# Hybrid decoder step on one core: output projection and first norm by single token groups, and two fixed PSUM banks for the inner down projections

## The chip, the core and the metric

The kernel runs on one core of one Trainium2 chip. The metric is the device time of one execution in microseconds (us). Before the change it is 2619.73 us, the median of 3 runs (2619.33 to 2625.12). The engines are named as in the profile: PE (TensorE matmul), PEld (its weight loads), DVE (VectorE), ACT (ScalarE), POOL (GpSimd), SP (SyncE, which issues most DMAs).

## The reference, cut to what matters

One layer of a decoder: an input projection, sliding-window attention beside an mLSTM, and then the part that this change touches, for 2048 prompt tokens and 64 sample tokens of width 1024 (the inner width of the FFN is 2816):

```python
def mix_and_ffn(x, att, h_m, o_pre, ...):
    o = jax.nn.sigmoid(o_pre).reshape(h_m.shape)
    y = jnp.concatenate([head_norm(att, g_attn), head_norm(o * h_m, g_mlstm)], axis=-1)
    x1 = layer_norm(DEEPNORM_ALPHA * x + y @ w_out, ln1_g, ln1_b)      # output projection, first norm
    ffn = (jax.nn.silu(x1 @ w_gate) * (x1 @ w_up)) @ w_down            # gate, up and down projection
    return layer_norm(DEEPNORM_ALPHA * x1 + ffn, ln2_g, ln2_b)         # second norm
```

Every matmul is done in float32 accuracy from split operands: a value is the sum of a rounded high part and a low part, and a product is three matmuls (high x high, high x low, low x high).

## The kernel before, in words

**Tiles.** Activations lie with the features on the 128 partitions (8 feature tiles, `KD`) and the tokens along the free axis. The 2112 tokens are cut into 4 *pairs* of *token groups*; a group has 256 tokens in pairs 0 and 1 and 272 in pairs 2 and 3 (`WH`), so a pair is 512 or 544 wide (`W2`). A pair is what the FFN works on: gate and up projection are done by one Strassen step, whose 2x2 right-hand matrix has the two groups of the pair as its columns and the two halves of the features as its rows. Its seven products P1 to P7 need the operands B11 (first features, first group), B21 (last features, first group), B22 (last features, second group) and the sums T1 to T4, which mix both groups. P1 needs B11 alone and P2 B21 alone; P3 needs B22; P4 to P7 need T4, T1, T2 and T3.

**Stages of one pair.** (1) `out_proj(g, m)`, m = 0 to 7: the output projection of feature tile m, 24 matmuls for each column range; a pair of 512 is one column range in one PSUM bank, a pair of 544 is two of 272. DVE adds the product to the residual (L1140), and POOL sums the eight tiles for the mean (L1125, L1127). (2) `ln1(g)`: the first norm. A mean by one matmul (L1151), subtraction (L1157, DVE), squares (L1159, ACT) and their sums, a reciprocal root (small DVE steps between L497 and L509 on PE), scaling (L1172, DVE), the bias (L1212, ACT), and then the Strassen operands, each split in high (L133, ACT) and low part (L142, DVE). For a pair of 512 all of it runs over the whole pair; for 544 the statistics run twice, one column half after the other, both after the eight products. (3) Strassen gate and up projection in 11 steps of two products sets, with (4) `down` between: after every 4 of the 22 inner tiles (`SLICES`) the down projection of those tiles is added to the residual (L1331), 8 feature tiles at a time; the last slice has 6 tiles. (5) `ln2`: the second norm and the output, run in the background of the next pair's first products.

**Weights.** `wblock` brings a 128x512 block of weights by one DMA (256 KB) on SP's queue, and ACT (L133) and DVE (L142) split it. `run` asks for five blocks ahead of the item in hand (`LOOK`), and there are 12 buffers for split weights and 5 for raw ones.

**PSUM.** Products of this part use four banks: two with the tag "ga", one "gb", one "gc". `gps()` deals them out in turn ("ga", "gb", "ga", "gc"). The Strassen products hold "ga", "gb" and "gc" by name, and when an inner `down` runs, P3 and P4 of the last set are still to come, so that one "ga" bank and "gc" hold sums that wait for them.

**Order.** At the end of pair g the items stand so: `begin(g + 1)` (loads of the residual and of the mixer's output Y), `out_proj(g + 1, 0)`, P3 and P4 of the last set, `out_proj(g + 1, 1..7)`, then the eight `down` items of the last slice of pair g, and behind each of them one or two steps of the generator `ln1(g + 1)` (`LSTEP`); what is left of it is drained behind the last `down`. For pair 0 there is no earlier pair: `out_proj(0, 0..7)`, the whole `ln1(0)`, then five "late" tiles of the input projection, which do not depend on it. The mixer (attention and mLSTM) of later tokens runs as a background queue between the products (`pace`, `bg_step`). Instructions are then put in order engine by engine by a scheduler that simulates the program as it is built; every engine executes its own list in that order.

## Time and profile before

| what | value |
|---|---|
| runs shown | 2619.73 us median (2619.33 to 2625.12) |
| profiled execution, its own time | 2622.01 us |
| its span on the core | 2619.6 us |
| PE busy | 2445.0 us (93%), 16383 matmuls |
| PE weight loads | 2234.3 us (85%) |
| DVE busy | 1688.2 us (64%) |
| ACT busy | 1171.4 us (45%) |
| POOL busy | 365.1 us (14%) |
| mean granted TensorE clock | 0.97 |
| HBM read, written | 339.26 MB, 68.06 MB |

The busy time of PE has a modelled end for each matmul, so that rows of neighbouring matmuls overlap: the distance from start to start says more of their cost than the duration does. A row such as `L145 PE MATMUL gps<-x,w` is one of the three matmuls of a split product (L145, L146, L147); `x` are the operands of the output projection and of gate and up, `h` those of the down projection. What stands in square brackets in a timeline row is the idle time of the engine before it and what ended it.

### The profile page before, as it was taken

Reading aid. Unit: us, or ns where it says so; the run is one execution under the profiler, and the core shown is the slowest. Engines: PE = TensorE matmul, PEld = TensorE weight load, DVE = VectorE, ACT = ScalarE, POOL = GpSimd, SP = SyncE. Lnnn points to the kernel's source line nnn. Section 1 sums busy time; section 2 is a strip of 40 time slices with the busy share of each in tenths; the row PEclk is TensorE's granted clock in tenths of the full one; section 3 lists DMA queues with packets and bytes.
Section 4 is the critical chain, followed back from the end, with each engine's and each line's share of the span. In section 5 each row is a group of like instructions: output and inputs, shape, how many; then the busy total and the mean of one; then the engine's idle time right before and its main releaser. Section 6 shows DMA issues by size and latency. Waiting matters only on the chain.

```text
span 2619.6 us, 44985 instructions
## 1 busy us (share of the span) xinstructions
PE 2445.0 (93%) x16383; PEld 2234.3 (85%) x16383; DVE 1688.2 (64%) x3956; ACT 1171.4 (45%) x2533; POOL 365.1 (14%) x391
## 2 busy tenths in 40 slices
PE   8999899977899999998999999789999998899996
PEld 8999777756888888878888899688999998899996
DVE  5224443555767766778766776866667748666666
ACT  3112433544454555545555463443444625454454
POOL 3322333202000000041000003110000021100002
PEclk9999999978999999999999999899999998999998
DMA  8643766642555555424655563256444623444453
GB/s 292 219 159 133 243 225 195 214 159 91 168 161 153 161 154 159 151 83 141 223 150 149 157 184 109 84 184 171 130 123 140 189 83 98 126 146 141 142 149 111
DMA packets 302712, 409.30 MB, mean 156 GB/s; under 512 B 31442, under 2 KB 172842, under 8 KB 302474
## 3 DMA queue, kind: packets, MB, share of 16 engines
q1 hardware_dynamic: 260240, 351.54, 44.7%
q10 hardware_dynamic: 42250, 54.89, 5.8%
q8 instruction: 128, 2.10, 0.3%
q14 instruction: 94, 0.77, 0.1%
HBM read 339.26 MB, written 68.06 MB: 155 GB/s over the span
## 4 chain that ended last, share of the span: by engine, by line
PE 45%; DVE 4%; DMA 3%; ACT 2%; issue 1%; POOL 1%; ACTq 0%; SPq 0%; DVEq 0%; POOLq 0%
PE gps L145 14%; PE gps L146 13%; PE gps L147 13%; DVE z L1172 1%; PE bps L571 1%; DMA P<-GW 1%; DMA x<-YD 1%; DVE w L142 1%; ACT w L133 1%; DVE z L1331 1%; DVE z L1157 0%; POOL ft L1164 0%; DMA out_oS<-P 0%; PE bps L596 0%; DMA z<-in_xT 0%
## 5 line engine op out<-in xcount | busy, mean ns | idle before, releaser
L133 ACT CAST w<-wr 128x512 fp32r<-128x512 f32 (+1 forms) x898 | 543.6, 611 | 842.3 <-PE gps L146 746.6
L145 PE MATMUL gps<-x,w 128*128 128x272 f32 (+3 forms) x2968 | 866.3, 301 | 55.9 <-ACT x L133 27.1
L146 PE MATMUL gps<-x,w 128*128 128x272 f32 (+3 forms) x2968 | 873.3, 297 | 7.3 <-DVE x L142 7.1
L147 PE MATMUL gps<-x,w 128*128 128x272 f32 (+3 forms) x2968 | 861.7, 296 | 2.5 <-DVE w L142 2.5
L142 DVE TENSOR_TENSOR w<-wr,w 128x512 fp32r<-128x512 f32 (+1 forms) x898 | 634.9, 714 | 217.9 <-ACT w L133 189.7
L145 PEld LDWEIGHTS gps<-x,w 128*128 128x128 f32 x2968 | 559.4, 191 | 87.5 <-ACT x L133 34.0
L146 PEld LDWEIGHTS gps<-x,w 128*128 128x128 f32 x2968 | 565.9, 191 | 20.4 <-DVE x L142 11.3
L147 PEld LDWEIGHTS gps<-x,w 128*128 128x128 f32 x2968 | 560.6, 191 | 14.3 <-DVE w L142 3.7
L145 PE MATMUL gps<-h,w 128*128 128x272 f32 (+1 forms) x1056 | 348.0, 333 | 21.1 <-DVE z L1331 13.8
L146 PE MATMUL gps<-h,w 128*128 128x272 f32 (+1 forms) x1056 | 342.2, 325 | 0.2 <-DVE h L142 0.2
L147 PE MATMUL gps<-h,w 128*128 128x272 f32 (+1 forms) x1056 | 341.3, 325 | 0.0
L145 PEld LDWEIGHTS gps<-h,w 128*128 128x128 f32 x1056 | 198.9, 189 | 46.9 <-DVE z L1331 20.8
L1331 DVE SCALAR_TENSOR_TENSOR z<-z,gps 128x272 f32<-128x272 f32 (+1 forms) x240 | 123.1, 518 | 146.4 <-PE gps L147 145.7
L147 PEld LDWEIGHTS gps<-h,w 128*128 128x128 f32 x1056 | 199.3, 189 | 15.7 <-issue 0.2
L146 PEld LDWEIGHTS gps<-h,w 128*128 128x128 f32 x1056 | 200.2, 190 | 13.5 <-DVE h L142 0.4
L142 DVE TENSOR_TENSOR x<-x 128x426 fp32r<-128x426 f32 (+3 forms) x72 | 51.6, 717 | 121.8 <-ACT x L133 102.2
L703 POOL TENSOR_SCALAR_AFFINE_SELECT P<-P 128x512 f32<-128x512 f32 x16 | 15.7, 979 | 808.3 <-DMA P<-GW 709.4
L1127 POOL TENSOR_TENSOR zs<-zs,z 128x512 f32<-128x512 f32 (+2 forms) x58 | 83.5, 1441 | 128.5 <-DVE z L1140 57.5
L196 POOL TENSOR_TENSOR st<-sa 128x256 f32<-128x256 f32 x88 | 66.3, 774 | 218.0 <-DMA SW<-st 181.4
L1164 POOL TENSOR_TENSOR ft<-ft 128x272 f32<-128x272 f32 (+1 forms) x56 | 60.7, 1083 | 254.2 <-ACT ft L1159 201.6
L133 ACT CAST x<-x 128x426 fp32r<-128x426 f32 (+3 forms) x72 | 42.1, 585 | 107.6 <-DMA x<-in_xT 59.1
L1125 POOL TENSOR_TENSOR zs<-z 128x512 f32<-128x512 f32 (+2 forms) x10 | 13.1, 1314 | 498.5 <-DVE z L1331 258.4
(340 smaller groups left out, 3600.5 us busy)
## 6 DMA issues: line engine op xcount, KB each, us to landing
wr<-SW SPq DMA_DIRECT2D x352, 256.0 KB, 2.8
wr<-in_wd SPq DMA_DIRECT2D x168, 256.0 KB, 2.9
wr<-in_wg SPq DMA_DIRECT2D x132, 256.0 KB, 2.7
wr<-in_wu SPq DMA_DIRECT2D x132, 256.0 KB, 2.8
SW<-st ACTq DMA_DIRECT2D x44, 512.0 KB, 5.3
wr<-in_wo SPq DMA_DIRECT2D x64, 256.0 KB, 2.9
sa<-in_wg SPq DMA_DIRECT2D x22, 512.0 KB, 4.8
sa<-in_wu SPq DMA_DIRECT2D x22, 512.0 KB, 4.7
```

Source lines behind the costliest of these rows:

```text
L133: A.copy(out, src)
L142: return veng.tensor_tensor(out=lo, in0=src, in1=hi.bitcast(F32), op=ALU.subtract)
L145: PE.matmul(out, lhsT=wh, rhs=xh, start=start, stop=False, **kw)
L146: PE.matmul(out, lhsT=wh, rhs=xl, start=False, stop=False, **kw)
L147: PE.matmul(out, lhsT=wl, rhs=xh, start=False, stop=stop, **kw)
L196: G.tensor_tensor(out=t[:, i], in0=x, in1=y, op=op)
L571: PE.matmul(s[g][:, j, 0:nk], lhsT=x[r, 2 * tt + j, :], rhs=y[r, 0:nk], start=(i == 0), stop=(i == 2))
L703: G.affine_select(out=gm, in_=gm, pattern=[[0, 4], [1, 128]], compare_op=ALU.is_ge, fill=BIG, base=0, channel_multiplier=-1)
L1127: G.tensor_tensor(out=s[:, c], in0=s[:, c], in1=z[m][:, c], op=ALU.add)
L1164: (V if len(qs) > 1 else G).tensor_tensor(out=q, in0=q, in1=t[:, 0:w], op=ALU.add)
L1172: return V.scalar_tensor_tensor(out=z[k][:, c], in0=z[k][:, c], scalar=Q[:, col + k:col + k + 1], in1=ry[:, 0:c.stop - c.start], op0=ALU.m ...
L1331: V.scalar_tensor_tensor(out=zm, in0=zm, scalar=ALPHA if s == 0 else 1.0, in1=p, op0=ALU.mult, op1=ALU.add)
```

## The change

The unit of the output projection and of the first norm becomes the single token group. `load_y`, `out_proj` and the statistics of `ln1` take one group (256 or 272 columns). All eight feature tiles of the first group are projected, then Y of the second group is loaded (`second`) and `ln1` is created; the eight tiles of the second group follow, with the steps of `ln1` for the first group behind them. The last-slice `down` items carry the rest, two steps each. A `wo` block that served a whole pair is now loaded and split once for each group. Y and the operands B11, B21 and B22 of a group keep their high and low part in one buffer. In `down`, the inner slices (`then` is None) alternate between the tags "ga" and "gb", and no longer take "gc".

```diff
-LSTEP = [2, 1, 1, 1, 1, 1, 2, 2]
+LSTEP = [2, 1, 1, 1, 1, 1, 1, 0]
...
-        def load_y(g):
-            c0, w = F0[g], W2[g]
+        def load_y(g, i):
+            c0, w = F0[g] + i * WH[g], WH[g]
             out = []
             for k in range(KD):
-                raw, h, l = x_tile(F32), x_tile(), x_tile()
+                raw, t = x_tile(F32), x_tile()
                 SP.dma_start(out=raw[:, 0:w], in_=YD[:, k, c0:c0 + w])
-                split("a", h[:, 0:w], l[:, 0:w], raw[:, 0:w])
+                h, l = t[:, 0:w], t[:, HW:HW + w]
+                split("a", h, l, raw[:, 0:w])
                 out.append((h, l))
...
-        def out_proj(g, m, fast=False):
+        def out_proj(g, i, m, fast=False, then=None):
             def fn(wa, wb):
-                z, y, s = P[g]["z"], P[g]["y"], P[g]["s"]
-                for o, n in cols(W2[g]):
-                    c = slice(o, o + n)
-                    p = gps()
-                    ys = [(h[:, c], l[:, c]) for h, l in y]
-                    product(p[:, 0:n], wa, ys[0:4], True, False)
-                    product(p[:, 0:n], wb, ys[4:8], False, True)
-                    V.scalar_tensor_tensor(out=z[m][:, c], in0=z[m][:, c], scalar=ALPHA, in1=p[:, 0:n],
-                                           op0=ALU.mult, op1=ALU.add)
+                z, y, s = P[g]["z"], P[g]["y"][i], P[g]["s"]
+                c = half(g, i)
+                p = gps()[:, 0:WH[g]]
+                product(p, wa, y[0:4], True, False)
+                product(p, wb, y[4:8], False, True)
+                V.scalar_tensor_tensor(out=z[m][:, c], in0=z[m][:, c], scalar=ALPHA, in1=p,
+                                       op0=ALU.mult, op1=ALU.add)
                 if not fast or m < KD - 1:
-                    add_to(s, z, m, slice(0, W2[g]))
+                    add_to(s, z, m, c)
+                if then is not None:
+                    then()
...
-            cc = [slice(o, o + n) for o, n in cols(W2[g])]
-            for i, c in enumerate(cc):
...
-            for k in range(4):
-                for kk in (k, k + 4):
-                    scale(z, kk, cc[-1], ry, Q_L1G)
...
+            for c in (a, b):
                 ry = yield from norm(z, c, P[g]["s"], gps, fast)
...
+                for k in range(KD):
+                    scale(z, k, c, ry, Q_L1G)
+                    A.activation(out=z[k][:, c], in_=z[k][:, c], func=AF.Identity, bias=Q[:, Q_L1B + k:Q_L1B + k + 1])
+                    if c is a:
+                        hl1("B11" if k < 4 else "B21", x1[k], k % 4, z[k][:, a])
...
                 hl2("U", k, t[:, 0:2 * w], ("T3", "T4"))
+                hl1("B22", x1[8 + k], k, z[k + 4][:, b])
...
-                    p = gps()[:, 0:c.stop - c.start]
+                    turn[0] += 1
+                    p = (gps() if then else gtag("ga" if turn[0] % 2 else "gb"))[:, 0:c.stop - c.start]
...
+        def second(g):
+            P[g]["y"].append(load_y(g, 1))
...
-            out_proj(0, m, True)
...
+            out_proj(0, 0, m, True)
+        ln0 = [None]
+
+        def begin_ln0():
+            second(0)
+            ln0[0] = ln1(0, True)
+        item(begin_ln0)
+        for m in range(KD):
+            out_proj(0, 1, m, True, step(ln0, LSTEP[m]))
...
-                out_proj(g + 1, 0)
+                out_proj(g + 1, 0, 0)
                 strassen(prev, "P3")
                 strassen(prev, "P4")
                 for m in range(1, KD):
-                    out_proj(g + 1, m)
+                    out_proj(g + 1, 0, m)
 
                 def tails(g=g, lngen=lngen):
-                    P[g]["zs"] = zsum()
+                    second(g + 1)
                     lngen[0] = ln1(g + 1)
                 item(tails)
                 for m in range(KD):
-                    down(g, s, m, cc, True, KD, step(lngen, LSTEP[m]))
+                    out_proj(g + 1, 1, m, False, step(lngen, LSTEP[m]))
+
+                def tails2(g=g):
+                    P[g]["zs"] = zsum()
+                item(tails2)
+                for m in range(KD):
+                    down(g, s, m, cc, True, KD, step(lngen, 2))
```

Three places show how the change moves instructions. The first is DVE's list at the boundary into pair 1. `z_...` are the residual tiles, `gps_...` the PSUM tiles, `w_...` the split weights. Before, the last product of the projection is added at full width, the first `down` product (L1331) follows, and only then the subtraction of the mean (L1157) begins:

```order
L1140 SCALAR_TENSOR_TENSOR z_11102<-z_11102,gps_11500 128x512
L142 TENSOR_TENSOR w_11530<-wr_11528,w_11529 128x256
L142 TENSOR_TENSOR w_11536<-wr_11534,w_11535 128x512
L1331 SCALAR_TENSOR_TENSOR z_5156<-z_5156,gps_11540 128x512
L142 TENSOR_TENSOR w_11607<-wr_11605,w_11606 128x256
L1157 TENSOR_TENSOR z_11088<-z_11088,gps_11588 128x512
```

Now the subtraction for the first group (L1162 in the new numbering) stands among the additions of the second group's products (L1143) and their weight splits:

```order
L1162 TENSOR_TENSOR z_11528<-z_11528,gps_12051 128x256
L142 TENSOR_TENSOR w_12070<-wr_12068,w_12069 128x512
L1143 SCALAR_TENSOR_TENSOR z_11516<-z_11516,gps_12080 128x256
L142 TENSOR_TENSOR w_12076<-wr_12074,w_12075 128x512
L1143 SCALAR_TENSOR_TENSOR z_11518<-z_11518,gps_12134 128x256
L142 TENSOR_TENSOR w_12124<-wr_12122,w_12123 128x512
L1169 TENSOR_TENSOR ft_12108<-ft_12108,ft_12111 128x256
L142 TENSOR_TENSOR w_12130<-wr_12128,w_12129 128x512
```

The norm of the first group has moved ahead of the `down` items and shares DVE with the second half of the projection.

The second place is PE's list where the last reciprocal root of the first norm is spread over the partitions (L509), at the boundary into pair 3. Before, the last `down` product stands ahead of it and Strassen products of the new pair (operands `x`) directly behind it:

```order
L147 MATMUL gps_24162<-h_23144,w_23971 128x272
L1151 MATMUL bps_24632<-zs_23603,avg_80 128x272
L509 MATMUL gps_24183<-C_76,rs_24116 128x68 x4
L145 MATMUL gps_24266<-x_23656,w_23976 128x272
L145 MATMUL gps_24366<-x_23656,w_24261 128x272
```

Now `down` products (operands `h`) stand behind it; nine of them, 18 matmuls each, follow that row (three of 512 columns at the boundaries into pairs 1 and 2):

```order
L147 MATMUL gps_25100<-h_24113,w_24932 128x272
L509 MATMUL gps_25075<-C_76,rs_25008 128x68 x4
L145 MATMUL gps_25162<-h_23452,w_24937 128x272
L146 MATMUL gps_25162<-h_23453,w_24937 128x272
L147 MATMUL gps_25162<-h_23452,w_24938 128x272
```

The work that PE has left when the norm's last factor is known has moved from none to nine products there.

The third place is an inner `down` of pair 3 on PE. Before, 4 of its 16 products stand among the next Strassen products, since their bank comes free only behind P3 or P4; one of them, between two Strassen products:

```order
L147 MATMUL gps_25290<-x_23671,w_25218 128x272
L145 MATMUL gps_25032<-h_24566,w_24872 128x272
L146 MATMUL gps_25032<-h_24567,w_24872 128x272
L147 MATMUL gps_25032<-h_24566,w_24873 128x272
L145 MATMUL gps_25032<-h_24609,w_24872 128x272
```

Now the products follow each other, here the end of one and the beginning of the next:

```order
L146 MATMUL gps_23014<-h_22932,w_22893 128x272
L147 MATMUL gps_23014<-h_22931,w_22894 128x272
L145 MATMUL gps_23028<-h_22542,w_22893 128x272
L146 MATMUL gps_23028<-h_22543,w_22893 128x272
L147 MATMUL gps_23028<-h_22542,w_22894 128x272
```

They alternate between one "ga" bank and "gb".

43 lines of the change are left out of this document (18 added, 25 removed).

## The prediction

> **What bounds the kernel now.** I read the page first, then tables by stage, then the waits of PE in the stages that are not full. The page's engine rows and its chain of work (PE's part is its first number):
>
> ```profile
> PE 2445.0 (93%) x16383; PEld 2234.3 (85%) x16383; DVE 1688.2 (64%) x3956; ACT 1171.4 (45%) x2533; POOL 365.1 (14%) x391
> PE 45%; DVE 4%; DMA 3%; ACT 2%; issue 1%; POOL 1%; ACTq 0%; SPq 0%; DVEq 0%; POOLq 0%
> ```
>
> PE is full over most of the span, so time can come only from where it is not. The tables by stretch (start:end, length, busy of PE, PEld, DVE, ACT, POOL, granted clock, DMA share, GB/s) show where: pair 0's projection and norm, and the three boundaries into pairs 1, 2 and 3.
>
> ```profile
> 505.00:563.00 58.00, 41.83 (x200) 28.30 (x196) 32.22 (x127) 23.04 (x63) 1.71 (x2) 0.74 0.34 104
> 563.00:622.00 59.00, 54.26 (x246) 40.88 (x247) 37.69 (x94) 26.90 (x63) 11.89 (x8) 1.00 0.60 195
> 622.00:662.00 40.00, 17.47 (x81) 15.61 (x80) 29.72 (x64) 20.53 (x38) 4.42 (x3) 0.70 0.13 39
> 1098.00:1129.00 31.00, 31.00 (x134) 25.07 (x134) 13.62 (x19) 6.66 (x13) 9.22 (x6) 1.00 0.28 81
> 1129.00:1160.00 31.00, 31.00 (x142) 25.01 (x142) 24.36 (x44) 11.42 (x22) 11.45 (x8) 1.00 0.32 91
> 1160.00:1200.00 40.00, 30.41 (x185) 26.67 (x185) 38.40 (x69) 23.50 (x45) 13.52 (x3) 0.87 0.29 91
> 1640.00:1700.00 60.00, 44.53 (x237) 37.72 (x237) 51.04 (x117) 28.37 (x57) 9.07 (x8) 0.80 0.25 76
> 2110.00:2180.00 70.00, 70.00 (x569) 69.61 (x567) 42.30 (x95) 19.83 (x42) 24.91 (x25) 1.00 0.28 83
> 2180.00:2220.00 40.00, 29.41 (x198) 27.24 (x197) 35.34 (x82) 23.76 (x45) 2.52 (x3) 0.83 0.31 93
> ```
>
> In each boundary PE is idle while DVE is nearly full (38.40 of 40 us), and in the stretch before it DVE is half idle (13.62 of 31 us) under a full PE. What PE waits for there, by the waits of PE in 622:662, 1640:1700, 2180:2220, and over the whole span, then in two inner down projections of pair 3 (2256:2284, 2410:2424):
>
> ```profile
> PE bps L145 <- ACT ev L939: 15.8, 1, 15.8
> ...
> PE gps L145 <- ACT x L133: 7.2, 3, 5.5
> ...
> PE gps L145 <- ACT x L133: 5.6, 2, 4.9
> ...
> PE gps L145 <- DVE z L1331: 13.9, 27, 2.1
> ...
> PE gps L145 <- DVE z L1331: 4.2, 4, 2.1
> ...
> PE gps L145 <- DVE z L1331: 1.6, 3, 0.5
> ```
>
> The first is a late tile whose bank ACT empties only behind the whole norm; the next two are Strassen operands that the norm has not made yet; the last three are products that wait until DVE has emptied their PSUM bank.
>
> **The change part by part.**
>
> *Pair 0.* Before, the projection needs all of Y of 512 tokens. These rows are the last Y written of the first 256 tokens and of the second, the first and last read of it, the split of the last, then the norm's subtraction, its scaling, and ACT's release of the late tile:
>
> ```profile
> 475.51 0.46 SPq L655 DMA_DIRECT2D YD<-ys  x1
> 574.66 0.38 SPq L655 DMA_DIRECT2D YD<-ys  x1
> 578.43 0.33 SPq L1106 DMA_DIRECT2D x<-YD  x1
> 588.92 0.43 SPq L1106 DMA_DIRECT2D x<-YD  x1
> 592.46 0.69 DVE L142 TENSOR_TENSOR x<-x 128x512 fp32r<-128x512 f32 x1 [2.30 <-ACT x L133]
> 628.40 4.87 DVE L1157 TENSOR_TENSOR z<-z,gps 128x512 f32<-128x512 f32 x8 [1.68 <-PE gps L1154]
> 645.91 5.36 DVE L1172 SCALAR_TENSOR_TENSOR z<-z,Q,gps 128x512 f32<-128x512 f32 x8 [2.17 <-PE gps L509]
> 661.01 1.21 ACT L939 ACTIVATE ev<-bps,C 128x424 f32<-128x424 f32 x2
> ```
>
> Now the first group's eight products (192 matmuls) use Y of 256 tokens, of which the last was written at 475.5; four of them stand ahead of the mixer's last steps in 505 to 563, where PE idles 16 us. Y of the second group needs 16 buffers instead of 24 of the 22, so that its four last reads need not follow each other at 3.5 us (578.43 to 588.92 in three steps): I put the last split at 586 instead of 593. From there DVE's list up to the second norm holds 26 us of work (26 splits, 16 additions and subtractions of 256, 8 scalings, one reciprocal root), and I add 4 us of waits: the second norm begins at 616 instead of 628.4, a gain of 12. From there to ACT's release the trace takes 32.6 us; at half width the subtraction costs 8 x 0.36 instead of 8 x 0.61 us, the scaling 8 x 0.42 instead of 8 x 0.67, the squares and splits some 2 us less: a gain of 6. Together 18 us. The late tiles and first Strassen products behind it are the same work. Bounds: 6, if the four early products (96 matmuls at 0.118, 11.3 us) delay the mixer by what does not fit its gaps; 28, if the 15.8 us wait goes with the 12.
>
> *Narrower matmuls.* A pair of 512 columns had 192 matmuls of 512 and has 384 of 256; pairs 2 and 3 keep theirs at 272. First and last row of a run of each (93 and 46 steps), in output projection and gate:
>
> ```profile
> 600.53 0.40 PE L147 MATMUL gps<-x,w 128*128 128x512 f32 x1
> ...
> 621.99 0.39 PE L147 MATMUL gps<-x,w 128*128 128x512 f32 x1
> ...
> 678.47 0.28 PE L147 MATMUL gps<-x,w 128*128 128x256 f32 x1
> ...
> 683.90 0.28 PE L145 MATMUL gps<-x,w 128*128 128x256 f32 x1
> ```
>
> That is 21.46 / 93 = 0.2308 us and 5.43 / 46 = 0.1180 us: 384 x 0.1180 - 192 x 0.2308 = 1.0 us for a pair, 2 us for two. The Trainium skill ("TensorE: Matmul & The Clock Gate", section "Back-to-back issue gap") speaks against the halving: for a sustained stream with weight loads it gives about 81 ns at 128 columns and 131 ns at 512. An estimate by it, with 98 ns at 256, makes each split matmul 65 ns dearer, 25 us for the two pairs. The trace does not agree with it: 512 columns take 0.2308 us here, and the halves nearly half.
>
> *Weights twice.* 64 more blocks, 16 for a pair. Rows by form on ACT and DVE, the additions, scalings and subtractions by width, the operand splits and the DMA:
>
> ```profile
> L133 ACT CAST w<-wr 128x512 fp32r<-128x512 f32 x858 | 528.0, 621 | 817.7 <-PE gps L146 726.4 <-PE gps L147 19.8 <-PE bps L146 15.0
> L142 DVE TENSOR_TENSOR w<-wr,w 128x512 fp32r<-128x512 f32 x858 | 615.1, 723 | 215.9 <-ACT w L133 187.7 <-PE gps L146 5.4 <-issue 4.9
> L1140 DVE SCALAR_TENSOR_TENSOR z<-z,gps 128x272 f32<-128x272 f32 x32 | 13.4, 433 | 19.9 <-PE gps L147 19.9
> L1172 DVE SCALAR_TENSOR_TENSOR z<-z,Q,gps 128x272 f32<-128x272 f32 x32 | 13.4, 491 | 1.1 <-PE gps L509 1.1
> L1172 DVE SCALAR_TENSOR_TENSOR z<-z,Q,gps 128x512 f32<-128x512 f32 x16 | 10.7, 743 | 2.4 <-PE gps L509 2.4
> L1157 DVE TENSOR_TENSOR z<-z,gps 128x272 f32<-128x272 f32 x32 | 11.5, 429 | 1.7 <-PE gps L1151 1.7
> L142 DVE TENSOR_TENSOR x<-ft,x 128x512 fp32r<-128x512 f32 x8 | 5.2, 676 | 0.0
> L1222 DVE TENSOR_TENSOR ft<-z 128x256 f32<-128x256 f32 x4 | 1.7, 416 | 0.0
> wr<-in_wo SPq DMA_DIRECT2D x64, 256.0 KB, 2.9
> ```
>
> Busy time by count is 0.72 us of DVE for a block: 11.5 us a pair, and 0.62 us of ACT: 9.8 us. With the second reciprocal root and twice the start-up of narrow instructions DVE gets some 17 us more in a pair of 512 and 12 in one of 272. I cost this at nothing in the projection itself, under PE's 192 x 0.118 = 22.7 us a group: the first group needs 16 x 0.72 + 8 x 0.42 = 14.9 us of DVE. The second group carries the first norm as well (8 subtractions, 3 additions, a root, 8 scalings, 8 splits, 14 us): 29 us against 22.7, so 6 us run over, less what five blocks of prefetch (3.6 us) take ahead. If that cover is gone, weights come late and PE waits on DVE's split: that is the slower rival below. On SP the 16 more DMAs of a pair stand between reads of Y; 32 blocks in 45 us are 8.4 MB, 186 GB/s, below the 195 of 563 to 622, where PE is busy 54.26 of 59.
>
> *Boundaries.* What is lost there: idle 40 - 30.41, 60 - 44.53 and 40 - 29.41, together 35.7 us; and clock, at most 30.41 x 0.13 + 44.53 x 0.20 + 29.41 x 0.17 = 17.9 us, of which I take half, 9, since the mean clock also counts idle time. Now PE has left, when the last factor of the norm is known, three down products (3 x 18 x 0.2308 = 12.5 us) into pairs 1 and 2, nine of 272 (162 x 70 / 569 = 19.9 us) into pair 3, and P1 and P2 of two sets (48 matmuls, 5.7 us): 18.2 and 25.6 us. DVE then needs 8 x 0.42 + 16 x 0.42 + 8 x 0.65 + 4 x 0.42 = 17 us for the operands, and some 8.6 and 12 us for weights and sums of those products, 25.6 and 29 us, though the first operand is done long before the last. I leave 5, 5 and 3 us of idle and 2 of clock: 30 us gained. Bounds: 0 (DVE keeps the boundary as it is) and 45.
>
> *Inner down projections.* In pair 3 the waits on L1331 are 4.2 + 3 x 1.6 = 9.0 us (the other two inner down projections there have the same row as the last quoted); with two banks in turn DVE has one product, 12 x 0.123 = 1.5 us, to empty the other bank in 0.43. I leave 0.5 us for each of four: 7 us gained. Bounds 0 and the whole 13.9.
>
> *Sum.* 18 + 30 + 7 - 2 = 53 us. The profiled execution's span is 2619.6 us and its time 2622.0; this gives 2569 for such a one and, from the median of the runs, 2.3 us lower, 2567.
>
> **The rivals.** (a) *DVE keeps the boundaries.* For it: 38.40 of 40 us at the first of them, and 12 to 17 us of work added for each; against it: 24 us of DVE's idle time in 1098 to 1160. The 30 us fall away: 2597. (b) *More is gained*: the boundaries lose nothing any more (45), pair 0 gains 28, the inner ones 9: 2540. Against it: DVE's own need above. (c) *Slower.* Place: DVE's strict list from the last Y to the last operand of each pair. If its idle time there can't be used, because it falls where DVE waits for PE's products, the added 17 + 12 + 12 us lie on the path, pair 0's 18 are kept and the inner 7 as well: 2619.7 + 41 - 25 + 2 = 2638. It decides once PE's waits for `w` in the second group's projection pass some 6 us a pair. (d) *The change doesn't do what it says*: the mixer's last steps are delayed by the early products, and the boundaries stay as in (a): 6 + 7 - 2 gained, 5 eaten by new waits for Y's buffers, 2614 to 2619, about no change.
>
> **How the numbers follow.** A measurement tells about 0.3%, 8 us, from no change. Forecast 2550 to 2585: 0.50. (a): 0.20. (b): 0.15. (c): 0.08, with it a weight load that is not hidden in the narrow matmuls. (d): 0.07. The predicted time is 2567. The range 2536 to 2606 leaves out (c), most of (d) and a tail below (b). Faster 0.50 + 0.20 + 0.15 = 0.85, the same 0.07, slower 0.08.
>
> **What would show it.** PE's 15.8 us wait for `ev` falls to 8 to 14, and the second norm's subtraction of pair 0 begins 10 us or more earlier. In the three boundaries PE's idle time falls from 35.7 to about 13 us and the clock is over 0.9; waits for `x` from L133 fall below 3 us. The waits on the down sums fall from 13.9 to about 5. Matmuls of 256 columns in the projection step at 0.118. It is wrong if PE waits for `w` by more than 6 us a pair, if the last Y of pair 0 is split after 595, or if the stretch between the boundaries grows by itself.

## The result, and the profile after

| | median of the runs | profiled execution, span | matmuls | mean granted clock |
|---|---|---|---|---|
| before | 2619.73 us (2619.33 to 2625.12) | 2619.6 us | 16383 | 0.970 |
| after | 2594.75 us (2594.57 to 2597.71) | 2592.8 us | 16821 | 0.976 |

The ratio is 0.9902 with an interval of 0.9879 to 0.9924: 25 us faster, less than half of the 53 that were forecast (2567). The time lies inside the range, 2536 to 2606, and next to the number of rival (a), but not for that rival's reason: the boundaries gained and pair 0 did not. (Some matmul records are missing in both traces, more of them before, so the counts don't compare.) The engine row and the chain row of the page:

```profile
PE 2443.2 (94%) x16821; PEld 2253.5 (87%) x16821; DVE 1747.1 (67%) x4146; ACT 1215.6 (47%) x2693; POOL 389.5 (15%) x424
PE 76%; DMA 8%; DVE 7%; POOL 4%; ACT 3%; issue 2%; SPq 0%; ACTq 0%; POOLq 0%; DVEq 0%
```

DVE has 59 us more to do and ACT 44, as is to be expected of the second split of the output weights and the narrower pieces, while PE's busy time is the same within 2 us. (PE's part of the chain, 45% before and 76% after, can't be compared: the parts of the row of before add up to only 56% of the span, those after to all of it.) The stretches shown before, in pair 0 and at the boundaries (same columns):

```profile
505.00:563.00 58.00, 43.35 (x242) 31.45 (x244) 34.71 (x127) 26.88 (x70) 1.68 (x2) 0.77 0.41 128
563.00:622.00 59.00, 50.48 (x363) 45.50 (x360) 48.73 (x135) 30.94 (x77) 13.93 (x15) 0.90 0.65 208
622.00:662.00 40.00, 21.80 (x130) 20.28 (x129) 29.91 (x79) 21.14 (x51) 4.36 (x5) 0.76 0.23 67
1160.00:1200.00 40.00, 35.22 (x235) 31.51 (x235) 39.88 (x75) 24.03 (x50) 13.28 (x4) 1.00 0.42 128
1640.00:1700.00 60.00, 56.44 (x349) 49.52 (x348) 57.28 (x111) 32.50 (x69) 20.72 (x10) 1.00 0.39 119
2110.00:2180.00 70.00, 60.81 (x470) 58.81 (x470) 59.49 (x139) 33.06 (x73) 23.47 (x22) 0.98 0.31 90
2180.00:2220.00 40.00, 39.65 (x316) 39.34 (x314) 29.78 (x52) 24.74 (x51) 5.34 (x5) 1.00 0.58 172
```

At fixed times the later boundaries slide out of such windows, because the kernel is ahead of the old one by then. Cut at a mark that both kernels have (DVE's last addition for P2 of the 4th and of the 22nd Strassen set of each pair, L1294 before and L1293 after), the three boundaries before are

```profile
1067.25:1212.02 144.77, 135.18 (x729) 113.08 (x729) 108.06 (x200) 68.33 (x142) 34.19 (x17) 0.96 0.38 115
1546.59:1717.02 170.43, 152.81 (x1033) 138.45 (x1032) 129.63 (x305) 75.70 (x167) 32.23 (x26) 0.93 0.39 116
2078.95:2233.99 155.04, 140.04 (x1066) 136.39 (x1065) 107.92 (x227) 66.61 (x132) 29.09 (x27) 0.94 0.35 108
```

and after

```profile
1065.56:1209.58 144.02, 136.09 (x954) 123.43 (x953) 127.41 (x278) 81.96 (x187) 36.05 (x27) 0.99 0.49 148
1547.20:1705.32 158.12, 148.20 (x1005) 135.05 (x1004) 137.86 (x308) 87.02 (x202) 43.57 (x33) 0.96 0.50 151
2064.52:2209.50 144.98, 135.79 (x1066) 133.63 (x1065) 123.36 (x254) 78.83 (x168) 35.99 (x34) 0.99 0.48 145
```

The lengths are the first numbers behind the bounds. By stage, after minus before:

| to pair 0's 4th set | pair 0 inside | boundary 1 | pair 1 inside | boundary 2 | pair 2 inside | boundary 3 | pair 3 inside | end |
|---|---|---|---|---|---|---|---|---|
| +0.2 | -1.8 | -0.7 | +3.0 | -12.3 | -2.7 | -10.1 | -4.8 | +2.4 |

The sum is -26.8, the difference of the spans. Nearly all of it is two boundaries. Pair 0, for which 18 us were forecast, gave nothing, and its stretch 563 to 622 got worse: PE 50.48 busy instead of 54.26, at a clock of 0.90 instead of 1.00. Of PE's waits in 505 to 700 after the change:

```profile
PE bps L145 <- ACT ev L939: 11.0, 1, 11.0
PE gps L145 <- DVE z L1143: 5.3, 1, 5.3
...
PE gps L497 <- POOL ft L1169: 4.1, 1, 4.1
...
PE bps L145 <- ACT w L133: 2.6, 1, 2.6
```

The wait for `ev` did shrink, from 15.8 to 11.0, but two new ones stand beside it: 5.3 us for a bank (L1143) and 2.6 for weights (0.3 before). The 4.1 us for the sums of squares aren't new: before, POOL and DVE (L1164) cost 1.5 and 2.8 there. In order of time, with the engine's idle time in brackets: the wait for a bank, the last Y written, the last split of Y, first and last of 37 late-tile matmuls, the last projection matmul, the second norm's subtraction, its scaling, the operand splits behind it, and ACT's copy that lets the late tiles go on:

```profile
574.89 0.58 PE L145 MATMUL gps<-x,w 128*128 128x256 f32 x1 [5.31 <-DVE z L1143]
583.63 0.38 SPq L655 DMA_DIRECT2D YD<-ys  x1
598.40 0.41 DVE L142 TENSOR_TENSOR x<-x 128x256 fp32r<-128x256 f32 x1
620.44 0.46 PE L145 MATMUL bps<-xh,w 128*128 128x424 f32 x1 [2.63 <-ACT w L133]
633.75 0.36 PE L145 MATMUL bps<-xh,w 128*128 128x424 f32 x1
636.66 0.28 PE L147 MATMUL gps<-x,w 128*128 128x256 f32 x1
640.02 2.73 DVE L1162 TENSOR_TENSOR z<-z,gps 128x256 f32<-128x256 f32 x8 [1.82 <-PE gps L1159]
651.34 3.22 DVE L1177 SCALAR_TENSOR_TENSOR z<-z,Q,gps 128x256 f32<-128x256 f32 x8 [2.06 <-PE gps L509]
659.17 1.89 DVE L142 TENSOR_TENSOR x<-ft,x 128x512 fp32r<-128x512 f32 x3
661.62 1.11 ACT L939 ACTIVATE ev<-bps,C 128x424 f32<-128x424 f32 x2
```

The last Y comes 9 us later than before (583.63, 574.66 before), and the second norm begins at 640.0 instead of at the 616 of the forecast (628.4 before). Its own tail is shorter, as foreseen: 21.6 us from subtraction to copy, 32.6 before.

### The profile page after: what moved, and what is told of

The parts are those of the page before. It is cut to its first block, busy times and chain, and to the rows that moved or that the text cites. A ratio compares the mean times of both kernels' runs of the same rounds, so it can differ in the third digit from the quotient of the medians.

```text
span 2592.8 us, 46615 instructions
## 1 busy us (share of the span) xinstructions
PE 2443.2 (94%) x16821; PEld 2253.5 (87%) x16821; DVE 1747.1 (67%) x4146; ACT 1215.6 (47%) x2693; POOL 389.5 (15%) x424
## 4 chain that ended last, share of the span: by engine, by line
PE 76%; DMA 8%; DVE 7%; POOL 4%; ACT 3%; issue 2%; SPq 0%; ACTq 0%; POOLq 0%; DVEq 0%
PE gps L145 21%; PE gps L146 20%; PE gps L147 20%; DMA SW<-st 3%; PE bps L571 2%; POOL st L196 2%; PE bps L147 2%; PE bps L145 2%; PE bps L146 2%; DVE w L142 1%; POOL zs L1129 1%; PE bps L603 1%; DMA x<-in_xT 1%; PE bps L596 1%; DVE z L1177 1%
## 5 line engine op out<-in xcount | busy, mean ns | idle before, releaser
L133 ACT CAST w<-wr 128x512 fp32r<-128x512 f32 x962 | 583.1, 612 | 800.4 <-PE gps L146 721.9
L145 PE MATMUL gps<-x,w 128*128 128x272 f32 (+3 forms) x3096 | 897.1, 295 | 35.8 <-ACT ft L1297 21.5
L146 PE MATMUL gps<-x,w 128*128 128x272 f32 (+3 forms) x3096 | 893.0, 290 | 1.4 <-DVE x L142 1.4
L147 PE MATMUL gps<-x,w 128*128 128x272 f32 (+3 forms) x3096 | 884.2, 291 | 0.8 <-DVE w L142 0.6
L142 DVE TENSOR_TENSOR w<-wr,w 128x512 fp32r<-128x512 f32 x962 | 682.5, 716 | 210.7 <-ACT w L133 185.5
L145 PEld LDWEIGHTS gps<-x,w 128*128 128x128 f32 x3096 | 585.2, 190 | 59.8 <-ACT ft L1297 26.2
L146 PEld LDWEIGHTS gps<-x,w 128*128 128x128 f32 x3096 | 589.6, 190 | 9.2 <-DVE x L142 3.5
L147 PEld LDWEIGHTS gps<-x,w 128*128 128x128 f32 x3096 | 583.7, 190 | 6.3 <-DVE w L142 1.4
L145 PE MATMUL gps<-h,w 128*128 128x272 f32 (+1 forms) x1056 | 346.5, 331 | 20.7 <-DVE z L1331 14.4
L1331 DVE SCALAR_TENSOR_TENSOR z<-z,gps 128x272 f32<-128x272 f32 (+1 forms) x240 | 123.2, 517 | 138.2 <-PE gps L147 137.8
L147 PEld LDWEIGHTS gps<-h,w 128*128 128x128 f32 x1056 | 199.8, 189 | 15.5
L703 POOL TENSOR_SCALAR_AFFINE_SELECT P<-P 128x512 f32<-128x512 f32 x16 | 15.7, 980 | 873.5 <-DMA P<-GW 641.7
L142 DVE TENSOR_TENSOR x<-x 128x426 fp32r<-128x426 f32 (+3 forms) x104 | 59.8, 576 | 107.6 <-ACT x L133 88.9
L1129 POOL TENSOR_TENSOR zs<-zs,z 128x272 f32<-128x272 f32 (+2 forms) x81 | 102.6, 1268 | 194.6 <-DVE z L1143 87.3
L133 ACT CAST x<-x 128x426 fp32r<-128x426 f32 (+3 forms) x104 | 48.6, 467 | 104.0 <-DMA x<-in_xT 66.0
L1169 POOL TENSOR_TENSOR ft<-ft 128x272 f32<-128x272 f32 (+2 forms) x62 | 65.5, 1057 | 202.2 <-ACT ft L1164 199.1
L1127 POOL TENSOR_TENSOR zs<-z 128x272 f32<-128x272 f32 (+2 forms) x14 | 14.1, 1004 | 510.1 <-DVE z L1331 250.0
```

What stands on the lines that cost most here:

```text
L133: A.copy(out, src)
L142: return veng.tensor_tensor(out=lo, in0=src, in1=hi.bitcast(F32), op=ALU.subtract)
L145: PE.matmul(out, lhsT=wh, rhs=xh, start=start, stop=False, **kw)
L146: PE.matmul(out, lhsT=wh, rhs=xl, start=False, stop=False, **kw)
L147: PE.matmul(out, lhsT=wl, rhs=xh, start=False, stop=stop, **kw)
L1129: G.tensor_tensor(out=s[:, c], in0=s[:, c], in1=z[m][:, c], op=ALU.add)
```

## The experiments

Later runs were on other chips, on which the kernel before takes 2630 to 2636 us, so that each kernel is compared by its ratio to runs of the kernel before beside it.

| kernel (ratio to before) | us | ratio | interval |
|---|---|---|---|
| the change, three times | 2594.75, 2602.43, 2602.37 | 0.9902, 0.9881, 0.9885 | 0.9879-0.9924, 0.9862-0.9900, 0.9868-0.9902 |
| p0_before: pair 0 in the old order | 2602.78 | 0.9890 | 0.9875-0.9905 |
| p0_hold: early products behind the mixer | 2599.89 | 0.9880 | 0.9865-0.9896 |
| z_pool: residual loads off SP's queue | 2596.07 | 0.9874 | 0.9850-0.9898 |
| wo_once: no second weight load and split | 2592.55 | 0.9847 | 0.9830-0.9864 |
| pool_split: half of the second splits on POOL | 2607.72 | 0.9907 | 0.9883-0.9931 |
| late_behind: late tiles behind the projection | 2602.97 | 0.9876 | 0.9847-0.9905 |
| ev_own: another buffer ring for `ev` | 2598.80 | 0.9859 | 0.9837-0.9881 |
| ev_late: both of these, twice | 2590.29, 2591.59 | 0.9835, 0.9842 | 0.9814-0.9856, 0.9825-0.9859 |
| ev_before: that ring in the kernel before | 2629.11 | 0.9985 | 0.9973-0.9998 |
| p0_ev: p0_before with that ring | 2588.81 | 0.9829 | 0.9815-0.9843 |
| narrow: kernel before, products of 256 | 2655.44 | 1.0079 | 1.0048-1.0110 |
| down_gps: inner downs deal four banks again | 2602.85 | 0.9888 | 0.9869-0.9908 |
| turn_fix: last-slice downs use four banks | 2599.15 | 0.9881 | 0.9859-0.9902 |
| p0_ev_gps: p0_ev with down_gps | 2597.38 | 0.9844 | 0.9823-0.9865 |
| p0_ev_turn: p0_ev with turn_fix | 2577.39 | 0.9766 | 0.9749-0.9783 |

For pair 0 these are the marks by which the traces are compared, in us from SP's third write at L617, which all of them issue at 518 to 524 us. The last split and the first copy are taken at their end, the others at their start. The last column is the 97th Strassen matmul: from there on the work is the same in all.

| kernel | last Y written | last split of Y | last projection matmul | second norm's subtraction | first copy to `ev` | 97th Strassen matmul |
|---|---|---|---|---|---|---|
| before | 54.8 | 73.3 | 102.1 | 108.5 | 141.8 | 175.6 |
| after | 64.4 | 79.6 | 117.4 | 120.8 | 143.0 | 176.8 |
| p0_before | 55.2 | 73.8 | 102.6 | 109.0 | 142.2 | 176.1 |
| p0_hold | 55.1 | 68.2 | 118.1 | 123.5 | 145.8 | 179.9 |
| z_pool | 66.3 | 80.1 | 111.3 | 116.9 | 139.3 | 173.3 |
| wo_once | 64.4 | 78.2 | 110.9 | 115.6 | 137.2 | 172.0 |
| late_behind | 63.4 | 78.6 | 110.5 | 116.0 | 138.1 | 172.8 |
| ev_own | 64.1 | 79.2 | 117.6 | 122.9 | 114.8 | 162.5 |
| ev_late | 64.9 | 80.0 | 112.7 | 118.2 | 119.4 | 161.4 |
| ev_before | 54.8 | 75.2 | 103.8 | 110.2 | 111.5 | 160.6 |
| p0_ev | 55.1 | 74.1 | 102.5 | 108.9 | 110.1 | 159.7 |
| narrow | 54.8 | 73.0 | 113.5 | 119.1 | 151.6 | 186.4 |

### Is pair 0 worth anything? (p0_before)

Pair 0 keeps the old `load_y`, `out_proj` and `ln1`; everything else is as changed.

```diff
-            out_proj(0, 0, m, True)
...
+            out_proj_b(0, m, True)
...
+        item(lambda: [None for _ in ln1_b(0, True)])
```

> The changed kernel, but pair 0 keeps its old projection and first norm (512 columns, weights once); pairs 1 to 3 and the down banks stay as changed. Theory P (the prediction): the change gained 18 us in pair 0, so 2613 us. Theory Q (read from the two traces): pair 0 gained nothing, since gate and up begin at 678.3 before and 678.8 after; then 2592 to 2598 us, and the boundaries and down products alone carry the 25 us.

Measured 0.9890; the change itself gave 0.9881 and 0.9885 in later calls. By the table the gate is under way at 176.1 with the old order and 176.8 with the new one. So the new order of pair 0 is worth nothing: within some 6 us by the intervals, which hold what it does to later stages as well, and within 1 us by the marks.

### What delays it (p0_hold, z_pool)

In p0_hold the first group's products wait for the mixer's last transpose.

```diff
+        first_tr = state['tr']
...
-                product(p, wa, y[0:4], True, False)
-                product(p, wb, y[4:8], False, True)
+                if g == 0 and i == 0:
+                    with tc.issue_after(first_tr.ins):
+                        product(p, wa, y[0:4], True, False)
+                        product(p, wb, y[4:8], False, True)
...
```

> The changed kernel, with the first group's products of pair 0 put behind the transposes of the mixer's last head norm on PE (L651), so that none of them runs in the mixer's last steps. If they delay the mixer and that costs the time: the last write of Y goes back from 583.6 to about 575 us and the time falls by 5 to 8 us, to 2587 to 2590. If PE's own work from 575 us on sets the end of pair 0's projection: 96 matmuls (11.5 us) move into that stretch, the mixer comes 8 us earlier, and the time is the same or up to 5 us longer, 2594 to 2600.

The last Y is then back at 55.1 and its last split at 68.2, earlier than before the change: the early products are what holds the mixer up by 9 us. But the norm comes no earlier (123.5). In the windows of p0_hold behind the mixer (575:605 and 605:640) there is hardly anything left to take:

```profile
575.00:605.00 30.00, 30.00 (x229) 28.51 (x230) 23.71 (x57) 21.34 (x51) 5.75 (x6) 0.93 0.64 195
605.00:640.00 35.00, 34.81 (x260) 32.00 (x259) 29.67 (x68) 21.72 (x52) 10.49 (x11) 1.00 0.54 161
```

PE is full with sixteen narrow products that now all stand here. The two ways cost about the same (176.8 and 179.9 at the last mark): the products early, and the mixer waits; or the products late, and the norm waits.

In z_pool POOL issues pair 0's reads of the residual, which otherwise stand on SP's queue among writes of the mixer.

```diff
-                SP.dma_start(out=z[:, 0:w], in_=xT[:, k, P0 + c0:P0 + c0 + w])
+                (SP if g else G).dma_start(out=z[:, 0:w], in_=xT[:, k, P0 + c0:P0 + c0 + w])
```

> The changed kernel, with the eight residual reads z of pair 0 issued by POOL instead of SP. On SP they stand behind the write of the mixer's last attention block and are issued at 568.9; DVE empties the first four banks only at 574.4, and PE waits 5.3 us for them. If z's place in SP's list is what stops the projection: DVE's first addition at 535 to 550, PE's wait of 5.3 us gone, the remaining four products of the first group in the mixer's gaps, 5 to 10 us gained: 2585 to 2590. If these products only delay the mixer further: the wait goes, the last write of Y comes later, and the time stays at 2593 to 2597.

```profile
535.61 4.44 POOL L1118 DMA_DIRECT2D z<-in_xT  x8
575.61 0.41 DVE L1143 SCALAR_TENSOR_TENSOR z<-z,gps 128x256 f32<-128x256 f32 x1
```

The residual is read at 535.6, yet the first addition to it still comes at 575.6: the four early products hold their banks for 40 us since their additions stand in DVE's list behind the mixer's steps, not since data are missing. PE's wait for L1143 (5.3 us in the change, 6.6 here) follows from that. z_pool is 0.0007 under the change, which is no difference.

### The weights twice (wo_once, pool_split)

In wo_once the second group's items carry no weight blocks and take the ones at hand, those of the first group's last feature tile: neither the DMA nor the splits of their own blocks are done.

```diff
-            def fn(wa, wb):
+            def fn(*ws):
+                if ws:
+                    P[g]["w"] = ws
+                wa, wb = P[g]["w"]
...
-            item(fn, (wo[:, m, 0:512], 4), (wo[:, m, 512:1024], 4))
+            item(fn, *([] if i else [(wo[:, m, 0:512], 4), (wo[:, m, 512:1024], 4)]))
```

> The changed kernel, but the second group's products of each pair all use the last two weight blocks of the first group: 64 loads and 64 splits on ACT and DVE are left out, the matmuls stay. Theory P (the prediction): the second splits are hidden under PE, so the same time within 3 us of the changed kernel. Theory D (read from the trace: DVE is busy 38 of the 43 us before the second norm of pair 0 and 39.9 of 40 at the first boundary): DVE's 11.5 us a pair are on the path, in pair 0 and at the three boundaries; 6 to 10 us each, 25 to 40 us faster than changed, a ratio to before of 0.973 to 0.980.

0.9847 against 0.9881 for the change beside it: about 9 us, 4.8 of them in pair 0 (172.0 against 176.8 at the last mark) and 3 in the second boundary (-15.4 instead of -12.1 to -12.3). The first boundary is no shorter for it (-0.1 instead of -0.7 to -2.1). What the forecast put at nothing costs about a third of what the change gains; that is between the two expectations. In pool_split POOL instead of DVE makes the low part of one of the two blocks of each product of the second group (the new last value in the item):

```diff
-            item(fn, (wo[:, m, 0:512], 4), (wo[:, m, 512:1024], 4))
+            item(fn, (wo[:, m, 0:512], 4), (wo[:, m, 512:1024], 4, i > 0))
```

> The changed kernel, with the low part of one of the two weight blocks of each product of the second group made by POOL instead of DVE (8 of 16 a pair; 5.8 us of DVE a pair). Theory D: 3 to 5 us for each of the four places, 12 to 20 us faster than changed, unless POOL, which takes 1.05 us for an addition of 256 columns, is itself late: then PE waits for w and it is 0 to 10 us slower. Theory P: the same within 3 us.

0.9907: that way out is no cheaper, and more likely dearer (by 0.0026, the intervals overlap).

### What PE really waits for in pair 0 (late_behind, ev_own, ev_late, ev_before, p0_ev)

In the new order 37 late-tile matmuls stand on PE ahead of the last projection product, 17 of them ahead of the last two (620.4 to 633.8 in the rows above). late_behind puts them behind (`P["last"]` is the last matmul of a product):

```diff
+                P["proj"] = P["last"]
...
-                product(p[:, 0:wl_], wa, xq[0:4], True, False)
-                product(p[:, 0:wl_], wb, xq[4:8], False, True)
+                with tc.issue_after(P["proj"].ins):
+                    product(p[:, 0:wl_], wa, xq[0:4], True, False)
+                    product(p[:, 0:wl_], wb, xq[4:8], False, True)
```

> The changed kernel, with the late tiles' matmuls put behind the last product of pair 0's projection on PE. As changed, 37 of them (7.1 us) stand ahead of its last two products. If they push the second norm back: its subtraction begins 6 to 8 us sooner (122 to 124 us behind the mixer's transposes of the chunk before, where it was 129 to 132), but the norm's tail then has 7 us more of late work to cover it and PE still waits for ev: 0 to 6 us faster than changed. If the last two products wait for their weights anyway (DVE 38 of 43 us busy): PE idles there, the subtraction begins at 128 to 130, and the time is the same or 2 us slower.

It has its subtraction earlier, and so has wo_once, here the rows of the one and the other:

```profile
637.65 2.74 DVE L1163 TENSOR_TENSOR z<-z,gps 128x256 f32<-128x256 f32 x8 [1.34 <-PE gps L1160]
...
636.73 2.74 DVE L1165 TENSOR_TENSOR z<-z,gps 128x256 f32<-128x256 f32 x8 [0.78 <-PE gps L1162]
```

By its marks 4 to 5 us are saved in pair 0, but the ratio, 0.9876, can't be told from the change.

ev_own leaves the order alone and gives ACT's copies of the late tiles buffers of another ring. They had come from `ft`, whose seven buffers also hold the T operands that wait for their splits:

```diff
-        return b1["f"].tile([128, FW], F32, tag="ft", name="ev", bufs=FTB)
+        return b1["f"].tile([128, FW], F32, tag="h", name="ev", bufs=2 * max(SLICES))
```

> The changed kernel, with the copies of pair 0's late tiles (L939) put into free buffers of the ring h instead of the ring ft, whose seven buffers the first norm's squares and operands hold. If PE's wait of 11 us for ev behind the first norm of pair 0 is a wait for an ft buffer: the wait goes to under 2 us, late tiles and the first gate products fill the norm's tail, 8 to 11 us faster than changed, a ratio to before of 0.984 to 0.986. If ACT's list holds the copy (the 18 casts and biases of the norm ahead of it): the wait stays above 6 us and the time within 3 us of changed (0.988).

First and last copy in ev_own, and below them PE's longest wait in 640 to 700:

```profile
637.10 0.60 ACT L939 ACTIVATE ev<-bps,C 128x424 f32<-128x424 f32 x1
...
659.77 0.52 ACT L939 ACTIVATE ev<-bps 128x424 f32<-128x424 f32 x1
...
PE gps L145 <- ACT x L133: 2.9, 1, 2.9
```

The 11 us wait is gone; the new group order had only taken it from 15.8 to 11.0. The copies run during the norm, and the gate is under way 14 us earlier (162.5). ACT was not too busy for the copies. In the trace of the change it idles 8.6 us for the norm's scaling, and the copy follows behind the norm's work in its list:

```profile
651.85 3.30 ACT L1211 ACTIVATE z<-z,Q 128x256 f32<-128x256 f32 x8 [8.59 <-DVE z L1177]
```

Its place in that list came from the ring: with other buffers the first copy stands ahead of the norm's squares (L1164, from 646.5). ev_late is ev_own with late_behind:

> Both edits together, the late tiles behind the projection and their copies in buffers of their own. If both waits are what they seem: 10 to 16 us faster than changed (0.982 to 0.984 of before), the norm's tail filled by all five late tiles (23 us of matmuls). If DVE's chain sets the tail's end: no better than the buffers alone.

0.9835, and 0.9842 when run again, against 0.9885 for the change in that call: 11 us. To see whether the new group order matters once this wait is gone, the same ring went into the kernel before and into p0_before:

> The kernel before, with only the copies of the late tiles put into the ring h. The prediction put PE's 15.8 us wait down to a copy that stands behind the whole norm, and its release into the 18 us of the group order. If the wait is for an ft buffer: it goes without any group order, and the kernel before gains 10 to 15 us (0.994 to 0.996). If ACT's list holds it: no change.

> Pair 0 in its old order (512 columns, weights once) with the copies in the ring h, pairs 1 to 3 as changed. Against the run with the late tiles behind the projection it tells what the group order of pair 0 is worth once the ring ft is out of the way. If the group order pays then (the second norm's tail is 9 us shorter by the traces): 4 to 9 us slower than that run. If the doubled weights and the delayed mixer eat it anyway: the same or up to 4 us faster.

```profile
630.46 0.61 ACT L939 ACTIVATE ev<-bps,C 128x424 f32<-128x424 f32 x1
```

That is ev_before: with the old order the copies begin at 630, right behind the projection, and the gate is under way at 160.6, 15 us earlier than before. p0_ev has it at 159.7, ev_late (with the new order) at 161.4. The whole gain of pair 0 was to be had by a buffer tag, without any of the new order. It doesn't all arrive at the end, however: ev_before as a whole is only 0.15% faster (0.9985, 4 us). In its trace pair 0 is 17 us ahead at its 4th set, loses 7 of them again up to its 22nd, and 15 in the first slice of pair 2, which is probably a matter of the chip (last section). Where the 7 go wasn't found.

### Narrow products (narrow)

The kernel before, with the projection of pairs 0 and 1 as two ranges of 256:

```diff
-                for o, n in cols(W2[g]):
+                for o, n in [(0, WH[g]), (WH[g], WH[g])]:
```

> The kernel before, with the projection of pairs 0 and 1 in two products of 256 columns instead of one of 512 (same weights, same places). Prediction: 1.0 us for a pair, 2 us slower in all (0.08%). By the sum of matmul steps in the traces of the changed kernel, 2 us for a pair: 4 us slower. By the Trainium skill's rule on sustained streams ('TensorE: Matmul & The Clock Gate', 'Back-to-back issue gap'), 25 us slower (0.95%), an estimate from its figures.

```profile
597.46 0.39 PE L145 MATMUL gps<-x,w 128*128 128x256 f32 x1
...
631.70 0.28 PE L147 MATMUL gps<-x,w 128*128 128x256 f32 x1
```

These are the first and the last of 288 matmuls without a pause between them: 34.24 / 287 = 0.1193 us, close to half of 0.2308. By the pitch the halving costs 384 x 0.1193 - 192 x 0.2308 = 1.5 us a pair, near the 1.0 that was forecast. And yet the kernel is 20.8 us slower. 10.8 are in pair 0 at the last mark (186.4 against 175.6): from its first projection matmul (44.6) to its last takes 68.9 us instead of 57.5, with no more Y to wait for. The window 563:622 of narrow:

```profile
563.00:622.00 59.00, 52.94 (x356) 47.44 (x356) 33.64 (x94) 24.89 (x59) 9.72 (x7) 0.86 0.53 169
```

The granted clock there is 0.86 where the kernel before has 1.00, which is 8 us of the 59 at most (0.94 in ev_before, on another of the later chips, so that a part of it may be the chip's), and PE waits 5.0 us for splits of Y (L133, L142) between 563 and 632, where it waited 1.9. Over the whole kernel the runs have a mean clock of 0.9615, those of the kernel before on the same chip 0.9656, which is 11 of the 20.8 us at most. Why PE waits longer isn't shown. A bank then holds half as much work, so that the four banks cover less of the time until the late Y tiles come; that is a likely reading, and it wasn't tried by itself. Boundary 1 is 4 us longer, and 13.5 are in pair 2, where ev_before, which has no narrow products, loses as much (15.5): those are probably the chip's. (These stages are against the kernel before on the first chip and add up to 31 us; the 20.8 are against runs beside it.)

### The inner down projections (down_gps, turn_fix, p0_ev_gps, p0_ev_turn)

down_gps deals the four banks to all `down` products, as before the change:

```diff
-                    turn[0] += 1
-                    p = (gps() if then else gtag("ga" if turn[0] % 2 else "gb"))[:, 0:c.stop - c.start]
+                    p = gps()[:, 0:c.stop - c.start]
```

> The changed kernel with all down products dealt the four banks in turn, as before the change. Theory P: the two fixed banks of the inner products gained 7 us (0.27%), so 7 us slower than changed. By the idle time in the traces (stretches 1800 to 2050 and from 2300 on): 5 to 6 us, less what two banks cost in the last slice (up to 4 us): 1 to 6 us slower than changed.

PE's waits for the down sums and for the copies of the Strassen sums in the last part of pair 3: before (2240:2550), after (2225:2550) and down_gps (2225:2550):

```profile
PE gps L145 <- DVE z L1331: 9.8, 16, 2.1
PE gps L145 <- ACT ft L1298: 1.7, 1, 1.7
...
PE gps L145 <- DVE z L1331: 5.5, 6, 3.3
PE gps L145 <- ACT ft L1297: 5.3, 7, 0.9
...
PE gps L145 <- DVE z L1330: 9.4, 13, 3.1
PE gps L145 <- ACT ft L1297: 1.7, 1, 1.7
```

The alternation takes 4.3 us from the waits for the down sums, and 3.6 us appear as waits of the next Strassen products for ACT's copies of their own banks: 11.5 before, 10.8 after, 11.1 with down_gps. The wait has moved. The whole span shows it too, and one thing more. These are the waits for the down sums in the change and, the edit below, in turn_fix:

```profile
PE gps L145 <- DVE z L1331: 14.4, 18, 3.3
...
PE gps L145 <- DVE z L1331: 7.9, 11, 3.3
```

Before they were 13.9, and they are 13.9 in down_gps: in the change they haven't fallen at all, because 7.2 us of them now stand in the three boundaries, where there were none. The alternation alone (down_gps to turn_fix) takes 6.0, and the waits for L1297 rise by 9.9 (15.7 to 25.6). As a whole, 0.9888 against 0.9881: 2 us, inside the interval.

The edit does one thing more. In the changed code a last-slice `down` steps the deal twice, once by `turn[0] += 1` and once within `gps()`, so that it uses two of the four banks, which is where the 7.2 us at the boundaries come from (1.3 there in turn_fix, 0.8 in down_gps); down_gps ends that too. turn_fix ends it and keeps the alternation of the inner ones, so that turn_fix against down_gps is the alternation alone:

```diff
-                    turn[0] += 1
+                    turn[0] += then is None
```

> The changed kernel, with the count that deals out PSUM banks stepped once for a last-slice down product instead of twice. As changed, it is stepped by two there, so that these products run on two banks only. If that makes PE wait for DVE at the boundaries (2.05 us at 1169.7, 0.8 + 1.9 + 1.3 at 2160 to 2169): 3 to 5 us faster than changed, 2590 to 2592. If DVE is the limit there anyway: the same, 2594 to 2596.

0.9881: no different from the change, nor from down_gps by more than 2 us. By stages boundary 3 gains (-16.7 instead of -10.1 to -12.3), and pair 1 loses (+6.6 instead of +3.0). The last two runs take p0_ev as their base:

> The best version so far (pair 0 in its old order with copies in the ring h, 0.9829 of before) with all down products dealt the four banks in turn, as before the change: only the boundaries of pairs 1 to 3 and the ring are left of all edits. The prediction gave 7 us (0.27%) to the two fixed banks of the inner products: 0.9856. By the waits of pair 3 (on the down sums 9.4 us with four banks, 5.4 with two; on the copies of the Strassen sums 1.7 and 7.0) the wait has moved: 0.9829 to 0.984.

> The best version so far, with the count stepped once for a last-slice product, so that these use four banks and the inner ones two. If the last slice's waits on two banks (2.0 us at the first boundary, 4.0 at the third) are on the path: 0.981 to 0.982. If DVE's norm sets the boundary: 0.9825 to 0.9835, no change.

p0_ev_turn is the fastest kernel: 0.9766, about 60 us faster than the kernel before beside it and 1.2% under the change. Here the alternation alone (p0_ev_gps, 0.9844, to p0_ev_turn) is worth 20 us: by stages pair 0 inside gives 9, pairs 1 and 3 some 6 each, pair 2 4. And four banks for the last slice alone (p0_ev, 0.9829, to p0_ev_turn) are worth 17 by the ratios, 9 by the two traces. Why the same edits do so much more here than on the change isn't settled. The deal goes on from where the projection left it, and a stage answers to that: boundary 2 gains 12.3 in the change, 4.4 in p0_before and again 4.4 in p0_ev, where only pair 0 is ordered otherwise, and 11.1 in p0_ev_turn. That points to the deal's position at the time; no run sets it by itself. In the page and the windows 622:662 and 2180:2220 of p0_ev_turn

```profile
PE 2440.8 (95%) x16601; PEld 2242.4 (87%) x16601; DVE 1726.0 (67%) x4079; ACT 1204.5 (47%) x2649; POOL 389.1 (15%) x415
622.00:662.00 40.00, 33.67 (x178) 31.11 (x176) 27.42 (x61) 19.60 (x36) 4.22 (x3) 0.89 0.52 162
2180.00:2220.00 40.00, 39.37 (x317) 38.89 (x316) 31.39 (x63) 26.01 (x54) 7.25 (x7) 1.00 0.59 168
```

PE is busy 33.7 of the 40 us in which it had 17.5 before and 21.8 after the change.

## Why the prediction was wrong, and where it held

**Pair 0: forecast +18 us, got none. This is the step that failed**, at two places. The first is "the second norm begins at 616". The sum counted DVE's work from the last split of Y on and took that split at 586; it came at 598.4, past the 595 that the prediction itself named as a sign of being wrong. From the split to the norm the sum had 30 us, and it took 41. The early products were allowed for only as a lower bound (6 us gained) if they "delay the mixer by what does not fit its gaps". They do: p0_hold gives the mixer its 9 us back. Beside it, the second group's weights (4.8 us, wo_once) and the late tiles (4 to 5 us, late_behind) stand in the way of the norm; the three overlap and don't add up. The second place is the reading under the quoted wait, "a late tile whose bank ACT empties only behind the whole norm". It took the order on ACT for the cause. The copy stood behind the norm because of its buffer of the `ft` ring; ev_before removes the wait with the norm where it was. "28, if the 15.8 us wait goes with the 12" was thus a bound on the wrong lever: 15 us are there, and the group order has no part in them. The sign "falls to 8 to 14" came true (11.0), but because the projection ended 15 us later and the wait began later with it, not because the norm came earlier. The "6 us" for the shorter tail were even too small (11 us from subtraction to copy), but a tail that starts 12 us late ends where it did.

**Weights twice: forecast nothing, measured about 9 us.** DVE's 6 us overrun in the second group was seen and then set against five blocks of prefetch. wo_once shows that the cover isn't there: PE's waits carry the name of the norm's or the mixer's steps, probably since the splits delay those in DVE's list, and only 2.6 us in pair 0 carry `w`. The sign that the prediction named for it, PE waiting for `w`, therefore didn't show it.

**Narrow products: forecast 2 us lost.** The pitch is as quoted (0.1193, against 0.118), so the reading of the rows holds, and the 25 us worked out from the Trainium skill ("TensorE: Matmul & The Clock Gate", section "Back-to-back issue gap") isn't confirmed as a cost of each matmul. But in the kernel before the halving did cost 20.8 us, 11 to 15 of them in the two stretches with narrow products, and up to 11 in the granted clock. A right unit price was used for the wrong question: the sum had no term for longer waits and the clock that goes with them. How much of this is in the changed kernel can't be told, since there the products meet other gaps.

**Boundaries: forecast +30, got 23.1** (0.7, 12.3 and 10.1 by the table; 25 to 26 in the two later runs of the change). The mechanism is right: PE's waits for operands `x` from L133 are gone there (over the whole span 27.1 us before, 4.3 after), and the clock rises from 0.96, 0.93 and 0.94 to 0.99, 0.96 and 0.99. PE's idle time in these stages falls from 9.6 + 17.6 + 15.0 = 42.2 us to 7.9 + 9.9 + 9.2 = 27.0, by 15; the forecast, in shorter stretches, had 35.7 fall to 13, by 23. What is missing stands at the first boundary, which gained next to nothing. Of the three it is the one to which the prediction's "DVE is nearly full" applies (38.40 of 40 us; 51.04 of 60 and 35.34 of 40 at the others), and DVE is as full after the change (39.88 of 40). But taking the second weight splits off DVE (wo_once) shortens it by nothing, so that the cause stays open. Rival (a) claimed that this would happen at all three.

**Inner downs: forecast +7, got 2 (turn_fix and down_gps, not told from zero).** In pair 3 the waits on L1331 fell as foretold (9.8 to 5.5), and most of the fall came back as waits for ACT's `ft` copies, a term that the sum did not have; the sign "from 13.9 to about 5" failed, because the last-slice products, left with two banks, took up what the inner ones gave (14.4 in all). The sum asked what a product waits for, and not what the next product waits for once that bank is taken twice. On p0_ev's order the same edit gives 20 us, so that the forecast's bounds, 0 and 13.9, were too narrow as well: a term for each wait can't see what the deal of the banks does to all later products.

**Sum.** 0 for pair 0, 23 for the boundaries, some 6 by stages inside the pairs (2 of them from the alternation), less 2.4 at the end: 27 in the trace, 25 in the runs. Rival (c) was wrong, since the added DVE work didn't outweigh the boundaries. Rival (d), "the mixer's last steps are delayed by the early products", was right for pair 0 alone, where it had only 7% with the boundaries tied to it.

## What to carry to other kernels

A wait for an engine's instruction is not yet a wait for that engine's other work: ask why the instruction stands where it does in the list, and above all from which ring its output buffer comes, before reordering whole stages; here one buffer tag gave the 15 us that a new stage order was meant to bring. Work that is moved into an engine's gaps is free only if everything ahead of which it is put has slack too, in program order on that engine and on the engine that must free its banks. And don't price a narrower tile by its pitch alone: here the pitch said 1.5 us a pair, and the kernel lost 20.8 in all, up to half of that with a lower granted clock.
